# Head norms of the second block's mixer, with the sums of squares made per head on a few partitions instead of per token

## The chip, the cores and the metric

One core of a Trainium2 chip runs one launch of the program. The metric is the device time in microseconds (us), the median of the runs. TensorE is called PE here, VectorE DVE, ScalarE ACT, GpSimd POOL; SP starts most DMAs.

## What is computed

Two transformer blocks of two layers each work on 512 tokens of 1024 features. The second block puts 16 meta tokens ahead (528 positions). Its mixer makes attention with a forget gate (8 heads), a convolution branch and a short convolution branch, and puts their outputs side by side: 1024 features, which are 16 groups ("heads") of 64. Each group is normalized by itself before the output product. The change touches this step alone:

```python
def head_rms_norm(y, g):
    b, l, d = y.shape
    yf = y.astype(jnp.float32).reshape(b, l, d // GROUP_HEAD_DIM, GROUP_HEAD_DIM)
    yf = yf * lax.rsqrt(jnp.mean(yf * yf, axis=-1, keepdims=True) + RMS_EPS)
    return (yf.reshape(b, l, d) * g.astype(jnp.float32)).astype(y.dtype)

def mixer_sublayer(h, pre_g, post_g, w_in, ...):
    ...
    y = jnp.concatenate([y_attn, y_conv, y_sc], axis=-1)
    y = jnp.einsum("ble,ed->bld", head_rms_norm(y, head_g), w_out)
    return h + rms_norm(y, post_g)
```

## The kernel before

Features lie on the partitions (8 tiles of 128 features, called c = 0 to 7, two heads in each), positions on the free axis, in two halves `H[0]` (positions 0 to 271) and `H[1]` (272 to 527). Every projection is made of three products of high and low float32r parts (`mm3`, lines 222 to 224), so PE is the engine with the most work. `mixer2` is called twice, once for each layer. Inside it, `pipeline` walks 20 attention units (scores, softmax, transposes, values); between them `fl.pump` puts in pieces of the projections that are still to be made, and `aux.pump(NORM[i])` puts in pieces of the head norms: `head_norm` is a generator, each of its `yield n` spends n of what a tick allows, and a tick allows 277. After the last unit a loop pumps what is left (`END`). The Tile scheduler then orders the instructions of each engine, so program order is only a start.

The attention outputs are left undivided by their softmax sums (`lrow`): a norm doesn't feel a factor for each token and head, except in its epsilon, so the epsilon is multiplied by the squared sum.

`head_norm(cs, hs)` is called for the tiles [0, 1], [2], [3] (once for each half), [4, 5] and [6, 7]. For each tile and half it squares (`hsq`, line 1423, ACT), and for each block of 128 tokens (and the 16 meta tokens) it takes the *squares as the stationary operand* and two columns of ones, `sel2`, as the moving one (line 1426): the sums arrive in the PSUM bank `x` with tokens on partitions, two columns for each tile. POOL has made `v` (the epsilon times the squared softmax sum, two columns at a time). DVE adds (line 1439), ACT takes the root (1441), DVE the reciprocal `hr` (1443), PE transposes it so that heads lie on partitions (1449), ACT and DVE split it into `rh` and `rl` (1451, 1452), a product with `sel` spreads each head's value over its 64 partitions (1458), and DVE multiplies (1462), ACT and DVE split the result for the output product (1465, 1466). There is one `x` bank: the sums, the transposes, the spread values, and the convolution branch's own products and statistics (1340, 326, 341, 222 with `ah`) follow each other in it. The output product (`out_proj`) of a tile and half begins when `y_done` has it.

Of the kernel before, what the change touches and what calls it, by code (L numbers as in the profile page):

```python
# [9 lines left out]
F32 = mybir.dt.float32  # L10
F32R = mybir.dt.float32r
# [13 lines left out]
RMS = 1e-6  # L25
# [13 lines left out]
MIX = 3  # L39
CT, HN = (260, 720, 617), (100, 160, 277)  # L40
END = (1050, 570)
# [38 lines left out]
def block_stack_kernel(ctx: ExitStack, tc: tile.TileContext, x_in, meta_in, vec_in, lam_in, wup1, wdn1, wqk1,  # L80
# [16 lines left out]

    small_bufs = {"mn": 8, "ls": 4, "rl": 4, "rt": 4, "rt_s": 4, "lf": 1, "lft": 1, "lfe": 1, "nl": 2, "hr": 3, "hv": 3, "lrow": 1, "lrowb": 1, "bl": 1, "bv": 1, "br": 1, "lame": 1}

# [9 lines left out]
    def bank(tag, shape=(128, 512)):  # L109
        return ps.tile(list(shape), F32, tag=tag, bufs=bank_tags[tag], name="ps_" + tag)  # L110
# [17 lines left out]
    epsc = one.tile([128, 2], F32, name="epsc")  # L128
    sel2 = one.tile([128, 2], F32, name="sel2")
    lamc = one.tile([128, 2 * DEPTH], F32, name="lamc")  # L130
# [690 lines left out]
    def mixer1(l, opnd, gpost, nxt):  # L821
        H = HALF[1]
        li = 0.8 - 0.6 * math.exp(-0.3 * l)
        with ExitStack() as st:
# [198 lines left out]
            def subln():  # L1023

                st_ = bank("t")
                for g in range(2):
                    sq = work("bsq")
                    act.activation(out=sq, in_=yb[g][:, T0:TALL], func=ACTF.Square)
                    for tb in range(4):
                        c = 8 * g + 2 * tb  # L1030
                        pe.matmul(out=st_[:, c:c + 2], lhsT=sq[:, tb * 128:tb * 128 + 128], rhs=sel2,
                                  start=True, stop=True)
# [87 lines left out]
    def mixer2(l, opnd, gpost, nxt):  # L1120
        H = HALF[2]
        TB = [(0, 16), (16, 144), (144, 272), (272, 400), (400, 528)]
        with ExitStack() as st:
# [285 lines left out]
            def head_norm(cs, hs):  # L1409

                while 2 * len(sel) < len(cs):
# [3 lines left out]
                    sel.append(t)  # L1415
                blocks = [(h, a, b) for h in hs for a, b in h.tb + ([(0, 128)] if h.meta else [])]
                nb, m = len(blocks), 2 * len(cs)
                stt = bank("x")
                v = small([128, 24], "hv")
                for i, c in enumerate(cs):  # L1420
                    for h in hs:
                        sq = half(name="hsq")
                        act.activation(out=sq[:, h.c], in_=Y(c)[:, h.g], func=ACTF.Square)
                        for j, (hb, a, b) in enumerate(blocks):
                            if hb is h:
                                pe.matmul(out=stt[:, m * j + 2 * i:m * j + 2 * i + 2], lhsT=sq[:, a - h.g0:b - h.g0],
                                          rhs=sel2, start=True, stop=True)
                    for j, (hb, a, b) in enumerate(blocks):

                        vo = v[:, m * j + 2 * i:m * j + 2 * i + 2]  # L1430
                        if c < 4:
                            qb = 0 if a == 0 else (a - 16) // 128 + 1
                            lq = lrow[:, 10 * c + qb:10 * c + qb + 6:5]
                            pool.tensor_scalar(out=vo, in0=lq, scalar1=RMS ** 0.5, scalar2=None, op0=ALU.mult)
                            pool.tensor_tensor(out=vo, in0=vo, in1=vo, op=ALU.mult)
                        else:
                            pool.memset(vo, RMS)
                yield HN[0] * len(cs)
                dve.scalar_tensor_tensor(out=v[:, :m * nb], in0=stt[:, :m * nb], scalar=1.0 / 64, in1=v[:, :m * nb],
                                         op0=ALU.mult, op1=ALU.add)  # L1440
                act.activation(out=v[:, :m * nb], in_=v[:, :m * nb], func=ACTF.Sqrt)
                r = small([128, 24], "hr")
                dve.reciprocal(out=r[:, :m * nb], in_=v[:, :m * nb])
                for h in hs:
                    rt = bank("x")
                    for j, (hb, a, b) in enumerate(blocks):
                        if hb is h:
                            n = 16 if a == 0 else 128
                            pe.transpose(rt[0:m, a - h.g0:a - h.g0 + n], r[0:n, m * j:m * j + m], ident[0:n, 0:n])
                    rh, rl = half(F32R, "rh"), half(F32R, "rl")  # L1450
                    act.activation(out=rh[0:m, h.c], in_=rt[0:m, h.c], func=ACTF.Copy)
                    dve.tensor_tensor(out=rl[0:m, h.c], in0=rt[0:m, h.c], in1=rh[0:m, h.c].bitcast(F32),
                                      op=ALU.subtract)
                    yield HN[1]
                    for i, c in enumerate(cs):
                        rb = bank("x")
                        for j, x in enumerate((rh, rl)):
                            pe.matmul(out=rb[:, h.c], lhsT=sel[i // 2][0:m, i % 2 * 128:i % 2 * 128 + 128],
                                      rhs=x[0:m, h.c], start=j == 0, stop=j == 1)
# [86 lines left out]

    pool.memset(onec, 1.0)
    pool.memset(zeroc, 0.0)
    pool.memset(epsc[:, 0:1], RMS)
# [13 lines left out]
    def load_rest(g0):  # L1563
# [4 lines left out]
        nc.scalar.dma_start(out=xT[:, :, 0:T0], in_=meta_in)  # L1568
        nc.scalar.dma_start(out=sel2, in_=c_selc[:, 8:10])
        cm = half(name="cm")  # L1570
# [220 lines left out]
```

## Time and profile before

| | |
|---|---|
| median of 3 runs | 3471.83 us (3468.62 to 3478.4) |
| profiled execution, its own time | 3497.96 us |
| span of the profiled execution | 3496.2 us, 56247 instructions |
| mean clock granted to TensorE | 0.971 of full speed |
| DMA | 291.42 MB, mean 83 GB/s |

The span is the time from the first to the last instruction; the 1.8 us between it and the execution's own time lie around it. The profiled execution is 26.1 us above the median of the runs. The clock is a share of 2.4 GHz: 1.00 is that level, 0.50 is 1.2 GHz, and a value between them is a stretch that had both.

### The profile page before, as it was taken

How to read it: one execution, taken by the hardware profiler on the slowest of the kernel's cores; microseconds unless marked ns; L12 is line 12 of the kernel's file. 1: busy time of each engine (PE TensorE's matmuls, PEld its weight loads, DVE VectorE, ACT ScalarE, POOL GpSimd, SP SyncE). 2: the span in 40 equal slices, each digit the busy share in tenths (PEclk: the TensorE clock that was granted, in tenths of full speed). 3: DMA queues.
4: the chain of work that ended last, by engine and by line, in shares of the span. 5: the costliest groups of instructions: out<-in, count | busy, mean ns of one | idle time of the engine just before them, and what ended most of it. 6: DMA issues, size and time to landing. Idle time of an engine off the chain costs nothing.

```text
span 3496.2 us, 56247 instructions
## 1 busy us (share of the span) xinstructions
PE 3447.2 (99%) x21851; PEld 3058.9 (87%) x21851; DVE 2033.9 (58%) x4429; ACT 1523.8 (44%) x3336; POOL 32.6 (1%) x147
## 2 busy tenths in 40 slices
PE   9999999999999999999999999999999999999998
PEld 8888988988898888878888898889999988899998
DVE  5442788744345432987644267548774486467743
ACT  6332566623244333666533344545443344554432
POOL 0000000000000000000000000000000000000000
PEclk9999999999999999999999999869999998799999
DMA  4233222232323332222223322102222221022222
GB/s 145 94 93 97 79 73 64 85 97 93 93 80 104 96 91 88 76 79 67 91 91 95 94 84 71 43 31 92 91 91 89 76 92 40 31 82 94 91 91 80
DMA packets 165819, 291.42 MB, mean 83 GB/s; under 512 B 19456, under 2 KB 36896, under 8 KB 165552
## 3 DMA queue, kind: packets, MB, share of 16 engines
q1 hardware_dynamic: 163648, 287.13, 26.2%
q8 instruction: 172, 2.82, 0.3%
q10 hardware_dynamic: 1904, 0.70, 0.1%
q14 instruction: 95, 0.78, 0.1%
HBM read 285.62 MB, written 2.13 MB: 82 GB/s over the span
## 4 chain that ended last, share of the span: by engine, by line
PE 89%; DVE 8%; ACT 2%; issue 1%; DMA 1%; SPq 0%; POOLq 0%; DVEq 0%; ACTq 0%
PE ps_acc L222 10%; PE ps_acc L224 10%; PE ps_acc L223 10%; PE ps_s L223 8%; PE ps_s L222 8%; PE ps_s L224 8%; PE ps_x L222 4%; PE ps_x L223 4%; PE ps_x L224 4%; PE ps_o L223 4%; PE ps_o L222 4%; PE ps_o L224 4%; PE ps_o L813 2%; PE ps_s L796 2%; DVE wl L201 1%; DVE y L1327 1%
## 5 line engine op out<-in xcount | busy, mean ns | idle before, releaser
L200 ACT ACTIVATE wh<-wr 128x512 fp32r<-128x512 f32 (+2 forms) x1068 | 616.9, 615 | 1110.9 <-PE ps_acc L223 488.2
L201 DVE TENSOR_TENSOR wl<-wr,wh 128x512 fp32r<-128x512 f32 (+2 forms) x1068 | 693.4, 673 | 470.2 <-ACT wh L200 457.9
L222 PE MATMUL ps_acc<-xh,wh 128*128 128x256 f32 (+2 forms) x1600 | 541.2, 338 | 1.1 <-DVE y L1303 0.7
L224 PE MATMUL ps_acc<-xh,wl 128*128 128x256 f32 (+2 forms) x1600 | 529.7, 331 | 0.0
L223 PE MATMUL ps_acc<-xl,wh 128*128 128x256 f32 (+2 forms) x1600 | 529.0, 331 | 0.0
L223 PE MATMUL ps_s<-xl,wh 128*128 128x512 f32 (+3 forms) x1088 | 360.6, 331 | 2.3 <-DVE xl L283 0.7
L222 PE MATMUL ps_s<-xh,wh 128*128 128x512 f32 (+3 forms) x1088 | 357.9, 329 | 0.9 <-DVE z L531 0.6
L224 PE MATMUL ps_s<-xh,wl 128*128 128x512 f32 (+3 forms) x1088 | 357.1, 328 | 0.0
L222 PEld LDWEIGHTS ps_acc<-xh,wh 128*128 128x128 f32 x1600 | 313.6, 196 | 30.6 <-issue 3.2
L224 PEld LDWEIGHTS ps_acc<-xh,wl 128*128 128x128 f32 x1600 | 313.9, 196 | 26.2 <-issue 0.8
L223 PEld LDWEIGHTS ps_acc<-xl,wh 128*128 128x128 f32 x1600 | 314.0, 196 | 22.7 <-issue 0.4
L223 PEld LDWEIGHTS ps_s<-xl,wh 128*128 128x128 f32 x1088 | 204.7, 188 | 25.5 <-DVE xl L378 5.2
L222 PEld LDWEIGHTS ps_s<-xh,wh 128*128 128x128 f32 x1088 | 204.7, 188 | 22.4 <-DVE z L531 1.1
L224 PEld LDWEIGHTS ps_s<-xh,wl 128*128 128x128 f32 x1088 | 204.7, 188 | 19.5 <-DVE wl L201 0.2
L222 PE MATMUL ps_x<-xh,wh 128*128 128x256 f32 (+3 forms) x608 | 204.8, 337 | 0.0
L223 PE MATMUL ps_x<-xl,wh 128*128 128x256 f32 (+3 forms) x608 | 202.4, 333 | 0.0
L224 PE MATMUL ps_x<-xh,wl 128*128 128x256 f32 (+3 forms) x608 | 202.0, 332 | 0.0
L223 PE MATMUL ps_o<-xl,wh 128*128 128x512 f32 (+3 forms) x544 | 180.0, 331 | 1.5
L222 PE MATMUL ps_o<-xh,wh 128*128 128x512 f32 (+3 forms) x544 | 177.8, 327 | 0.1
L224 PE MATMUL ps_o<-xh,wl 128*128 128x512 f32 (+3 forms) x544 | 177.5, 326 | 0.0
L223 PE MATMUL ps_acc<-hl,wh 128*128 128x256 f32 (+1 forms) x528 | 168.7, 319 | 0.0
L224 PE MATMUL ps_acc<-hh,wl 128*128 128x256 f32 (+1 forms) x528 | 168.3, 319 | 0.0
(348 smaller groups left out, 7672.5 us busy)
## 6 DMA issues: line engine op xcount, KB each, us to landing
wr<-in_wup_dram SPq DMA_DIRECT2D x528, 256.0 KB, 2.8
wr<-in_wdn_dram SPq DMA_DIRECT2D x192, 256.0 KB, 2.7
wr<-in_wqk_dram SPq DMA_DIRECT2D x96, 256.0 KB, 2.7
wr<-in_wdn_dram SPq DMA_DIRECT2D x96, 192.0 KB, 2.7
wr<-in_wo_dram SPq DMA_DIRECT2D x64, 256.0 KB, 2.7
wr<-in_wv_dram SPq DMA_DIRECT2D x40, 256.0 KB, 2.8
wr<-in_wcv_dram SPq DMA_DIRECT2D x40, 256.0 KB, 2.8
dec<-fdram SPq DMA_DIRECT2D x16, 264.0 KB, 4.4
```

The lines of the kernel that those rows point to most:

```text
L200: act.activation(out=hi[:, a:b], in_=raw[:, :b - a], func=ACTF.Copy)
L201: eng.tensor_tensor(out=lo[:, a:b], in0=raw[:, :b - a], in1=hi[:, a:b].bitcast(F32), op=ALU.subtract)
L222: pe.matmul(out=o, lhsT=wh[wsl], rhs=xh[xsl], start=start, stop=False)
L223: pe.matmul(out=o, lhsT=wh[wsl], rhs=xl[xsl], start=False, stop=False)
L224: pe.matmul(out=o, lhsT=wl[wsl], rhs=xh[xsl], start=False, stop=stop)
L796: pe.matmul(out=o, lhsT=a[R, qs], rhs=b[R, ks], start=j == 0, stop=j == 2 and mask is None)
L813: pe.matmul(out=o[:, q0:], lhsT=v, rhs=p[j], start=kb == 0 and j == 0, stop=kb == n - 1 and j == 1)
L1327: dve.scalar_tensor_tensor(out=y[:, s:], in0=t[0][:, :TALL - s], scalar=w[:, 30 - s:31 - s], in1=y[:, s:], op0=ALU.mult, op1=ALU.add))
```

## The change

Sums with heads on partitions. The squares are now the *moving* operand: `selz` is a tile of 16 columns, zero but for the two columns of ones in the middle, and a slice of it that begins at column 7 - 2i puts the sums of tile i of a call on rows 2i and 2i + 1 of the `x` bank, for all 272 (or 256) positions of a half in one product (line 1430); the other rows get zeros added. For the attention tiles, `v` (now one DVE instruction, 64 times the epsilon times the squared sums) is transposed and added in the same bank by a product with the identity, for each block of tokens (1434). ACT takes the root of that row block of up to 4 x 272 values out of PSUM, with 1/64 as scale and, for the tiles without softmax sums, the epsilon as bias (1436); DVE takes the reciprocal of those 4 x 272 values (1438); `rh` and `rl` are split from it (1440, 1441). The add on DVE, the transposes of the reciprocals and all of POOL's work on `v` are gone. `HN` is (277, 277, 277): each piece of a norm spends a whole tick. All squares of a call come in the first piece, then one piece for each half up to `rl`, and only then the spread products.

```diff
-CT, HN = (260, 720, 617), (100, 160, 277)
+CT, HN = (260, 720, 617), (277, 277, 277)
...
-                                pe.matmul(out=stt[:, m * j + 2 * i:m * j + 2 * i + 2], lhsT=sq[:, a - h.g0:b - h.g0],
-                                          rhs=sel2, start=True, stop=True)
...
-                            pool.tensor_scalar(out=vo, in0=lq, scalar1=RMS ** 0.5, scalar2=None, op0=ALU.mult)
-                            pool.tensor_tensor(out=vo, in0=vo, in1=vo, op=ALU.mult)
-                        else:
-                            pool.memset(vo, RMS)
-                yield HN[0] * len(cs)
-                dve.scalar_tensor_tensor(out=v[:, :m * nb], in0=stt[:, :m * nb], scalar=1.0 / 64, in1=v[:, :m * nb],
-                                         op0=ALU.mult, op1=ALU.add)
-                act.activation(out=v[:, :m * nb], in_=v[:, :m * nb], func=ACTF.Sqrt)
-                r = small([128, 24], "hr")
-                dve.reciprocal(out=r[:, :m * nb], in_=v[:, :m * nb])
+                m, attn, sqs, rr = 2 * len(cs), cs[0] < 4, {}, {}
+                if attn:
+
+                    v, lq = small([128, 20], "hv"), lrow[:, 10 * cs[0]:10 * cs[0] + 5 * m]
+                    dve.scalar_tensor_tensor(out=v[:, 0:5 * m], in0=lq, scalar=64.0 * RMS, in1=lq, op0=ALU.mult,
+                                             op1=ALU.mult)
                 for h in hs:
-                    rt = bank("x")
-                    for j, (hb, a, b) in enumerate(blocks):
-                        if hb is h:
-                            n = 16 if a == 0 else 128
-                            pe.transpose(rt[0:m, a - h.g0:a - h.g0 + n], r[0:n, m * j:m * j + m], ident[0:n, 0:n])
-                    rh, rl = half(F32R, "rh"), half(F32R, "rl")
-                    act.activation(out=rh[0:m, h.c], in_=rt[0:m, h.c], func=ACTF.Copy)
-                    dve.tensor_tensor(out=rl[0:m, h.c], in0=rt[0:m, h.c], in1=rh[0:m, h.c].bitcast(F32),
+                    for c in cs:
+                        sqs[c, h.i] = half(name="hsq")
+                        act.activation(out=sqs[c, h.i][:, h.c], in_=Y(c)[:, h.g], func=ACTF.Square)
+                yield HN[0]
+                for h in hs:
+                    ms, r = bank("x"), half(name="hr")
+                    for i, c in enumerate(cs):
+                        pe.matmul(out=ms[0:m, h.c], lhsT=selz[:, 7 - 2 * i:7 - 2 * i + m], rhs=sqs[c, h.i][:, h.c],
+                                  start=i == 0, stop=not attn and c == cs[-1])
+                    blocks = [(j, max(a, h.lo), b) for j, (a, b) in enumerate(TB) if h.lo <= a < h.hi]
+                    for j, a, b in blocks if attn else []:
+                        pe.matmul(out=ms[0:m, a - h.g0:b - h.g0], lhsT=v[:b - a, j:5 * m:5], rhs=ident[:b - a, :b - a],
+                                  start=False, stop=j == blocks[-1][0])
+                    act.activation(out=r[0:m, h.c], in_=ms[0:m, h.c], func=ACTF.Sqrt, scale=1.0 / 64,
+                                   bias=0.0 if attn else epsc[0:m, 0:1])
+                    dve.reciprocal(out=r[0:m, h.c], in_=r[0:m, h.c])
+                    rh, rl = rr[h.i] = half(F32R, "rh"), half(F32R, "rl")
+                    act.activation(out=rh[0:m, h.c], in_=r[0:m, h.c], func=ACTF.Copy)
+                    dve.tensor_tensor(out=rl[0:m, h.c], in0=r[0:m, h.c], in1=rh[0:m, h.c].bitcast(F32),
                                       op=ALU.subtract)
                     yield HN[1]
+                for h in hs:
                     for i, c in enumerate(cs):
                         rb = bank("x")
-                        for j, x in enumerate((rh, rl)):
+                        for j, x in enumerate(rr[h.i]):
...
+    pool.memset(selz, 0.0)
...
-        nc.scalar.dma_start(out=sel2, in_=c_selc[:, 8:10])
+        nc.scalar.dma_start(out=selz[:, 7:9], in_=c_selc[:, 8:10])
```

What moves, at three places of the first layer's mixer. The first is PE at the norm of the convolution tiles [4, 5]; before, its ten products of two columns (line 1426) stand in this piece of the order, among a unit's transposes and scores (L1285, L1288, L1291 transposes, L796 scores, L813 values).

```order
L1288 MATMUL ps_t<-ident,sc 16x16
L1426 MATMUL ps_x<-sel_84,hsq 128x2 x8
L1291 MATMUL ps_t<-ident,sc 128x128
L796 MATMUL ps_s<-ql,qh 128x400 x2
L1426 MATMUL ps_x<-sel_84,hsq 128x2 x2
L813 MATMUL ps_o<-pt,v 128x256 x8
```

In the changed kernel the sums of its first half stand earlier, among products of a projection (L222 to L224); those of the second half follow twenty rows below.

```order
L222 MATMUL ps_acc<-xh,wh 128x256
L1430 MATMUL ps_x<-hsq,selz 4x272
L1285 MATMUL ps_o<-ident,sc 16x128
L1430 MATMUL ps_x<-hsq,selz 4x272
L223 MATMUL ps_acc<-xl,wh 128x256
L224 MATMUL ps_acc<-xh,wl 128x256
L796 MATMUL ps_s<-qh 128x272 x2
```

Eight products in a row have become two, with a transpose between them.

The second place is PE at the norm of the tiles [0, 1]. Before, the transposes of the reciprocals (L1449) stand behind the scores of a unit.

```order
L796 MATMUL ps_s<-qh,ql 128x272 x2
L1449 MATMUL ps_x<-ident,hr 4x128 x2
L1449 MATMUL ps_x<-ident,hr 4x16
L813 MATMUL ps_o<-pt,v 128x272
L813 MATMUL ps_s<-pt,v 128x272
L796 MATMUL ps_s<-qh 128x256
L326 MATMUL ps_x<-onec,lacc 128x1 x3
```

In the changed kernel the sums of the second half (L1430, L1434), the convolution branch's transposes (L341, L343) and the first spread product (L1448) follow each other here in the one `x` bank.

```order
L1430 MATMUL ps_x<-hsq,selz 4x256 x2
L1434 MATMUL ps_x<-ident,hv 4x128 x2
L813 MATMUL ps_o<-pt,v 128x272 x2
L813 MATMUL ps_s<-pt,v 128x272 x2
L796 MATMUL ps_s<-qh 128x256
L341 MATMUL ps_x<-ident,R 128x128 x2
L343 MATMUL ps_x<-ident,R_21975 128x16
L813 MATMUL ps_o<-pt,v 128x256
L796 MATMUL ps_s<-ql,qh 128x256
L796 MATMUL ps_s<-qh,ql 128x256
L813 MATMUL ps_s<-pt,v 128x256
```

PE no longer waits for the reciprocal there; it asks for the `x` bank three times within a dozen rows.

The third place is DVE at the same norm, in the changed kernel alone (before, the reciprocal of 128 x 20 values stood between a unit's score reductions): the reciprocal of the second half stands ahead of the multiplication L1358, which reads the transposes L341 out of the `x` bank.

```order
L201 TENSOR_TENSOR wl<-wr,wh 128x512
L1438 RECIPROCAL hr<-hr 4x256
L1358 TENSOR_TENSOR y<-y,ps_x 128x272 x2
L1441 TENSOR_TENSOR rl<-hr,rh 4x256
L1298 TENSOR_TENSOR pt<-ps_t,pt 128x2x128 x2
```

So the bank is given up only behind that reciprocal.

On ACT the order of the changed kernel has 72 loads of a function table where that of before has 70.

## Rows read from the trace of the kernel before

**Rows 1.** The page, parts 1 and 4: busy time of each engine; the chain.
```profile
PE 3447.2 (99%) x21851; PEld 3058.9 (87%) x21851; DVE 2033.9 (58%) x4429; ACT 1523.8 (44%) x3336; POOL 32.6 (1%) x147
...
PE 89%; DVE 8%; ACT 2%; issue 1%; DMA 1%; SPq 0%; POOLq 0%; DVEq 0%; ACTq 0%
```
**Rows 2.** Windows: stretch, length, busy time of each engine, clock, DMA share, GB/s.
```profile
2112.00:2346.00 234.00, 221.71 (x1361) 190.47 (x1359) 134.48 (x375) 112.74 (x290) 12.25 (x62) 0.80 0.14 45
2834.00:3067.00 233.00, 220.65 (x1365) 189.57 (x1364) 135.08 (x377) 112.62 (x291) 12.13 (x61) 0.79 0.14 45
400.00:680.00 280.00, 275.61 (x1959) 240.39 (x1958) 232.59 (x610) 176.13 (x452) 0.00 (x0) 0.99 0.23 71
```
**Rows 3.** Windows: stretches of the second block's mixers, columns as in rows 2.
```profile
2222.00:2251.00 29.00, 26.64 (x117) 22.90 (x117) 13.85 (x42) 14.99 (x31) 0.41 (x2) 0.59 0.06 19
...
2265.00:2274.00 9.00, 9.00 (x48) 7.58 (x47) 1.74 (x9) 4.05 (x10) 0.97 (x13) 0.62 0.17 57
...
2283.00:2313.00 30.00, 30.00 (x129) 25.02 (x129) 12.98 (x40) 11.62 (x26) 0.41 (x2) 0.54 0.08 24
...
2319.00:2345.00 26.00, 22.84 (x96) 19.26 (x97) 7.77 (x20) 7.73 (x20) 0.00 (x0) 0.55 0.00 1
...
2988.00:2999.00 11.00, 11.00 (x59) 8.97 (x60) 2.91 (x11) 5.45 (x17) 1.56 (x16) 0.69 0.15 49
...
3005.00:3035.00 30.00, 29.95 (x130) 24.76 (x130) 13.15 (x42) 12.00 (x29) 0.41 (x2) 0.55 0.06 18
```
**Rows 4.** Timeline of PE: start, length, line, operands, shape, count.
```profile
2265.26 2.01 PE L1426 MATMUL ps_x<-sel,hsq 128*128 128x2 f32 x16
...
2283.72 0.51 PE L1426 MATMUL ps_x<-sel,hsq 128*128 128x2 f32 x4
...
2284.45 0.41 PE L224 MATMUL ps_acc<-xh,wl 128*128 128x256 f32 x1
```
**Rows 5.** Windows: the first block's mixer, a stretch of its first layer.
```profile
562.00:568.00 6.00, 6.00 (x36) 5.58 (x37) 4.31 (x16) 3.30 (x7) 0.00 (x0) 0.72 0.24 87
```
**Rows 6.** Groups of instructions, PE: count, busy us, mean ns, idle before.
```profile
L1426 PE MATMUL ps_x<-sel,hsq 128*128 128x2 f32 x160 | 23.0, 260 | 1.5 <-ACT hsq L1423 1.4
L1449 PE MATMUL ps_x<-ident,hr 128*4 128x128 f32 (+3 forms) x50 | 11.7, 324 | 5.5 <-DVE hr L1443 2.4 <-DVE y L1358 1.9 <-DVE y L1462 1.2
L1340 PE MATMUL ps_x<-y,onesm 128*128 128x272 f32 (+1 forms) x16 | 4.8, 399 | 0.0
L1031 PE MATMUL ps_t<-sel,bsq 128*128 128x2 f32 x32 | 4.2, 254 | 0.0
```
**Rows 7.** Waits of PE, both layers: us in total, times, longest.
```profile
PE ps_x L1449 <- DVE hr L1443: 2.4, 2, 1.2
...
PE ps_x L1449 <- DVE y L1358: 1.9, 2, 1.0
PE ps_x L1458 <- DVE rl L1452: 1.9, 2, 0.9
...
PE ps_x L1458 <- DVE y L1462: 1.2, 2, 0.6
PE ps_x L1449 <- DVE y L1462: 1.2, 2, 0.6
```
**Rows 8.** Groups of instructions, DVE, 2210 to 2350 us.
```profile
L1452 DVE TENSOR_TENSOR rl<-ps_x,rh 4x272 fp32r<-4x272 f32 x3 | 1.3, 429 | 3.4 <-ACT rh L1451 3.4
...
L1443 DVE RECIPROCAL hr<-hv 128x20 f32<-128x20 f32 x3 | 0.8, 274 | 0.3 <-ACT hv L1441 0.3
...
L1443 DVE RECIPROCAL hr<-hv 128x4 f32<-128x4 f32 x1 | 0.2, 178 | 0.3 <-ACT hv L1441 0.3
```
**Rows 9.** Timeline of ACT at the norm of the tiles [0, 1].
```profile
2217.92 0.22 ACT L1441 ACTIVATE hv<-hv 128x20 f32<-128x20 f32 x1 [1.37 <-DVE hv L1439]
2218.16 1.28 ACT L1241 ACT_TABLE_LOAD   x1
...
2220.73 0.39 ACT L1451 ACTIVATE rh<-ps_x 4x272 fp32r<-4x272 f32 x1 [0.55 <-PE ps_x L1449]
```

More of the change, by code (lines that the diff above doesn't have):

```diff
@@ L96, in half @@
         return hp.tile([128, HB], dt, tag="h", name=name)
-    small_bufs = {"mn": 8, "ls": 4, "rl": 4, "rt": 4, "rt_s": 4, "lf": 1, "lft": 1, "lfe": 1, "nl": 2, "hr": 3, "hv": 3, "lrow": 1, "lrowb": 1, "bl": 1, "bv": 1, "br": 1, "lame": 1}
+    small_bufs = {"mn": 8, "ls": 4, "rl": 4, "rt": 4, "rt_s": 4, "lf": 1, "lft": 1, "lfe": 1, "nl": 2, "hv": 3, "lrow": 1, "lrowb": 1, "bl": 1, "bv": 1, "br": 1, "lame": 1}
     def small(shape, name="sm"):
@@ L128, in block_stack_kernel @@
     epsc = one.tile([128, 2], F32, name="epsc")
-    sel2 = one.tile([128, 2], F32, name="sel2")
+    selz = one.tile([128, 16], F32, name="selz")
     lamc = one.tile([128, 2 * DEPTH], F32, name="lamc")
@@ L1030, in subln @@
                         c = 8 * g + 2 * tb
-                        pe.matmul(out=st_[:, c:c + 2], lhsT=sq[:, tb * 128:tb * 128 + 128], rhs=sel2,
+                        pe.matmul(out=st_[:, c:c + 2], lhsT=sq[:, tb * 128:tb * 128 + 128], rhs=selz[:, 7:9],
                                   start=True, stop=True)
@@ L1415, in head_norm @@
                     sel.append(t)
[L1416 to L1423, printed above, removed]
-                        for j, (hb, a, b) in enumerate(blocks):
-                            if hb is h:
-                                pe.matmul(out=stt[:, m * j + 2 * i:m * j + 2 * i + 2], lhsT=sq[:, a - h.g0:b - h.g0],
-                                          rhs=sel2, start=True, stop=True)
[L1428 to L1433, printed above, removed]
-                            pool.tensor_scalar(out=vo, in0=lq, scalar1=RMS ** 0.5, scalar2=None, op0=ALU.mult)
-                            pool.tensor_tensor(out=vo, in0=vo, in1=vo, op=ALU.mult)
-                        else:
-                            pool.memset(vo, RMS)
@@ L1438, in head_norm @@
-                yield HN[0] * len(cs)
-                dve.scalar_tensor_tensor(out=v[:, :m * nb], in0=stt[:, :m * nb], scalar=1.0 / 64, in1=v[:, :m * nb],
-                                         op0=ALU.mult, op1=ALU.add)
-                act.activation(out=v[:, :m * nb], in_=v[:, :m * nb], func=ACTF.Sqrt)
-                r = small([128, 24], "hr")
-                dve.reciprocal(out=r[:, :m * nb], in_=v[:, :m * nb])
-                for h in hs:
-                    rt = bank("x")
-                    for j, (hb, a, b) in enumerate(blocks):
-                        if hb is h:
-                            n = 16 if a == 0 else 128
-                            pe.transpose(rt[0:m, a - h.g0:a - h.g0 + n], r[0:n, m * j:m * j + m], ident[0:n, 0:n])
-                    rh, rl = half(F32R, "rh"), half(F32R, "rl")
-                    act.activation(out=rh[0:m, h.c], in_=rt[0:m, h.c], func=ACTF.Copy)
-                    dve.tensor_tensor(out=rl[0:m, h.c], in0=rt[0:m, h.c], in1=rh[0:m, h.c].bitcast(F32),
+                m, attn, sqs, rr = 2 * len(cs), cs[0] < 4, {}, {}
```

## The prediction

> **What bounds the kernel now.** I read the page first. PE is busy 99% of the span and carries 89% of the chain that ended last; DVE is busy 58%, ACT 44%, POOL 1% [rows 1]. So time comes out of PE's own work, out of its waits, or out of its clock, and work on DVE or ACT costs only where PE ends up waiting for it. The windows then show where PE is slow although it is busy. The two mixers of the second block take 234 and 233 us and had a granted clock of 0.80 and 0.79, while the first block's mixer, with the same kind of attention, had 0.99 [rows 2]. A stretch at 0.50 does half of its products; with PE busy, a stretch loses its length times (1 - clock): 234 x 0.20 + 233 x 0.21 = 95.7 us over both layers. That is much more than PE waits for there, and the head norms lie in just these stretches.
>
> Which stretches are they? In the first layer 2222 to 2251 (0.59), 2265 to 2274 (0.62), 2283 to 2313 (0.54) and 2319 to 2345 (0.55); the second layer repeats the middle two at 2988 (0.69) and 3005 (0.55) [rows 3]. In the first and the last of them PE has 2 to 3 us without work. In the middle two it has none: 9.00 of 9.00 and 30.00 of 30.00 us are busy. What PE did ahead of these is the burst of sums with two moving columns: sixteen passes from 2265.26, and the last four of another from 2283.72; a projection's product at 2284.45 is already at 0.41 us, the half-clock length [rows 4]. The first block has such sums too, line 1031, 32 passes in both layers [rows 6], and the one slow stretch of its first mixer, 562 to 568 at 0.72, lies right behind its share of them [rows 5]. I read from this that a row of products which move two columns each ends with the clock at 1.2 GHz, with no wait needed.
>
> **The change, part by part.** *PE's own work.* A float32 product appears as two passes in the trace, a transpose as one. Before, the sums are 160 passes with 23.0 us busy and the transposes 50 with 11.7 us [rows 6]: 34.7 us go. What comes: 16 tile-halves a layer, 32 products, 64 passes of 272 or 256 moving columns. Line 1340 moves the same columns in float32: 4.8 us for 16 passes, 0.30 each [rows 6], so 64 x 0.30 = 19.2 us. The stationary side has 4 columns instead of 128 there; I know of no row that prices this, and take no gain. And 30 products of `v` with the identity, 60 passes, 48 of them of 128 columns and 12 of 16. From below, 0.30 x 128 / 264 = 0.145 each, 8.7 us; from above the transposes of line 1449, which move 128 columns too, mostly at half clock: 11.7 / 50 = 0.234, 14.0 us. I take the middle, 11.4. Sum: 30.6 - 34.7 = -4 us. The bounds are -7 and, with the removed sums at the full-clock price of line 1031 (4.2 / 32 = 0.131, so 21.0 in place of 23.0), +1.
>
> *ACT.* 20 roots of 272 or 256 columns in place of 12 short ones. The nearest row of that width is `rh`, 0.39 us; a short root took 0.22 [rows 9]: 20 x 0.39 - 12 x 0.22 = +5.2 us, and two more table loads at 1.28 [rows 9] make +7.8. On an engine that is busy 112.7 of 234 us there [rows 2] this costs nothing by itself; without cover it would cost 7.8 us, which is inside the bound of the waits below. The root out of PSUM is also what frees the `x` bank.
>
> *DVE.* 20 reciprocals of 272 or 256 columns in place of 12 of 4 to 20. A reciprocal took 274 ns for 20 columns and 178 for 4 [rows 8], 6.0 ns a column, so about 178 + 268 x 6.0 = 1.79 us for 272 whatever the number of partitions. The other end is the subtraction in that shape, 0.43 us [rows 8], if the slope ended; I take 1.79, since the slope is between two rows of this very instruction. DVE gains about 20 x 1.74 - 12 x 0.25 = +32 us over both layers, at 57% busy in the mixers [rows 2]: hidden as work. What queues behind each reciprocal is hidden only if PE has something else to do.
>
> A rule of the Trainium skill speaks against this edit: by its page "VectorE: DVE Perf Modes", section "First, the fixed hardware budget", the reciprocal is an iterative division with a repeat count of 8. With the clock of 0.96 GHz of that page's "Specifications" this is an estimate of 272 x 8 / 0.96 = 2.27 us, where the slope of the rows gives 1.79. By the page DVE would gain 42 us instead of 32, and the slow case below would come out some 9 us later. The rows agree that the price goes with the columns and not with the partitions; they show a smaller step.
>
> *Waits.* Gone are PE's waits ahead of the transposes, 2.4 + 1.9 + 1.2 = 5.5 us in both layers [rows 7]. The chain from sums to `rl` is now root 0.39, reciprocal 1.79, `rh` 0.39, `rl` 0.43, 3.0 us, against 0.22 + 0.27 + 0.39 + 0.43 = 1.3 and the transposes [rows 8, 9], so up to 1.7 us longer, twenty times. Since each step of a norm now has a tick of its own, most have products of a projection in between. Where not: at the norm of [0, 1] the second half's sums, the branch's transposes and a spread product share the `x` bank within a dozen rows, and on DVE the reciprocal stands ahead of the multiplication that empties the bank. That is 1.7 + 2 x 0.43 = 2.6 us, with four products in between, at 0.41 us or less each [rows 4]: 1 to 2 us of wait, I take 1.5. At [4, 5] and at [2] the sums of the second half need the bank that the root of the first half still reads, with a table load of 1.28 us ahead of it; I take 1 us each, and 1 us at the norm of [6, 7] at the end: 4.5 a layer, 9 in all, less 5.5, +3.5 us. From below nothing new: -5.5. From above all twenty chains uncovered by 1.7 us: 34 - 5.5 = +28.5.
>
> POOL's `v` instructions go; nothing but the norm waited for them, so nothing changes there.
>
> *The clock.* With the bursts gone, the two middle stretches of each layer need not fall: 9 x 0.38 + 30 x 0.46 + 11 x 0.31 + 30 x 0.45 = 34.1 us is what they lose [rows 3]. But once the clock is down there it stays so through a mixture of values, transposes and spread products without a wait, and the new waits of about 1 us lie at the same places. No row shows what a stream of 272 columns past 4 stationary ones does to the clock. I take half, -17 us, between 0 and -34.
>
> **Sum.** -4 + 3.5 - 17 = -17.5 us. On the profiled execution's own 3497.96 us that is 3480; that execution lies 26 us above the median of the runs, 3471.83, on which the forecast is made: 3454 us.
>
> **Rivals.** *The clock falls all the same.* The waits at [4, 5] and [2] take the place of the bursts. The stretch 2222 to 2251, behind waits for the norm of [0, 1], speaks for it; against it, that only 1 us is meant to wait there. Time: -4 + 3.5, 3471 us.
>
> *The reciprocals hold PE up (slower).* One mechanism: reciprocals of 1.7 us on DVE between the sums and the next use of the one `x` bank. With no gain of clock and all chains uncovered: 28.5 - 4 = +24, 3496 us. It decides from 1.0 us uncovered per chain: 20 x 1.0 - 5.5 - 4 = +10.5. For it: one bank, and a DVE order that puts the reciprocal ahead of the instruction that frees it. Against it: DVE idles 43% of these stretches and the longer chain often has ten or more products beside it.
>
> *The clock holds nearly throughout.* If the streams keep it up, the stretches around 2222 and 2319 (29 x 0.41 + 26 x 0.45 = 23.6 us, doubled for the second layer 47) may shorten by half too: -34 - 24 + 3.5 - 4 = -58, 3414 us. Against it: these two have real waits, and the output product's last tile still needs its norm.
>
> **How the numbers follow.** 0.3%, 10.4 us, is about what a measurement of this kernel can tell from no change. Chances: the forecast (3440 to 3465) 0.36, the clock falls all the same 0.26, the reciprocals 0.26, the clock holds 0.12. Faster: most of the first and all of the last, 0.46; within 0.3%: most of the second with the edges of the first and third, 0.27; slower 0.27. The 80% range reaches into the last case and nearly to the full price of the reciprocals: 3420 to 3492 us.
>
> **What would show it.** Right: the sums as 64 passes of about 0.3 us or less; reciprocals near 1.8 us; no wait of PE for a reciprocal ahead of a transpose; clock well above 0.62 and 0.54 behind the norms of [4, 5] and [2]; PE waits of 1 us or so at the `x` bank for the root (1436) or for multiplications behind a reciprocal. Wrong: a clock of the mixers still near 0.80 (then the bursts were not the cause, or the waits have replaced them), or PE waits above 20 us in all on the norm's lines (then the reciprocal is the bound).

## The result, and the profile after

The changed kernel takes 3436.8 us (median of 4 runs, 3436.42 to 3440.26), beside 3475.11 for the kernel before on the same chip: a ratio of 0.989, 95% interval 0.986 to 0.992, or 38 us less. It is faster; the forecast was 3454, and 3436.8 lies 3 us below the forecast case's own 3440 to 3465 and inside the range of 3420 to 3492. The gain is twice the forecast one, 38 us for 17.5.

The page of the changed kernel, parts 1 and 4:

```profile
span 3434.7 us, 55936 instructions
...
PE 3384.3 (99%) x21765; PEld 2995.1 (87%) x21765; DVE 2061.5 (60%) x4433; ACT 1530.6 (45%) x3346; POOL 8.6 (0%) x28
...
PE 88%; DVE 8%; ACT 2%; issue 1%; DMA 1%; SPq 0%; POOLq 0%; DVEq 0%; ACTq 0%
```

PE is the bound as before [rows 1], and it is without work for 3434.7 - 3384.3 = 50.4 us of the span, against 3496.2 - 3447.2 = 49.0 before. So the waits have not become fewer. The windows show where the time came from: both mixers, then four stretches of the first.

```profile
2099.00:2309.00 210.00, 198.68 (x1377) 164.42 (x1376) 156.76 (x394) 119.28 (x302) 0.13 (x1) 0.94 0.17 53
2800.00:3001.00 201.00, 189.10 (x1288) 155.20 (x1288) 146.39 (x375) 114.94 (x294) 0.00 (x0) 0.93 0.16 52
2205.00:2231.00 26.00, 24.36 (x169) 18.75 (x167) 18.61 (x54) 22.80 (x51) 0.00 (x0) 1.00 0.06 21
2231.00:2240.00 9.00, 7.94 (x43) 6.92 (x42) 5.45 (x15) 5.71 (x14) 0.00 (x0) 0.62 0.19 60
2240.00:2296.00 56.00, 52.50 (x358) 39.77 (x354) 42.09 (x97) 38.88 (x92) 0.13 (x1) 1.00 0.12 38
2296.00:2307.00 11.00, 10.15 (x38) 8.22 (x38) 4.69 (x12) 4.07 (x12) 0.00 (x0) 0.54 0.00 0
```

The mixers' clock is 0.94 and 0.93 where it was 0.80 and 0.79 [rows 2]. The two stretches in the middle, behind the norms of [4, 5] and [2], which were at 0.62 and 0.54 [rows 3], are gone: 2240 to 2296 is at 1.00. What is left of long half-clock stretches in this mixer comes behind waits: 2231 to 2240 behind the waits of the convolution branch's products for the `x` bank and for their operand `al`, 2296 to 2307 behind those at the mixer's end. By length times (1 - clock) the mixers now lose 210 x 0.06 + 201 x 0.07 = 26.7 us, where they lost 95.7.

The profiled execution before was a long one (3497.96 us), so these two profiles differ by more than the medians do. For all runs there is a number that takes the clock out: span x mean granted clock is what the span would be at 2.4 GHz throughout, and the rest of it is what the clock took. The clock is given to three decimals, so one run is known to 2 us, a mean to about 1.

| kernel | median us | ratio to before, 95% | span x clock, mean | taken by the clock, mean |
|---|---|---|---|---|
| before (21 runs) | 3474.9 | | 3397 | 78 |
| changed | 3436.8 | 0.986 to 0.992 | 3396 | 40 |
| E1 before, products regrouped | 3481.8 | 0.999 to 1.003 | 3397 | 81 |
| E2 before, products 128 wide | 3443.7 | 0.988 to 0.992 | 3397 | 45 |
| E3 changed + narrow products | 3463.4 | 0.994 to 0.998 | 3412 | 49 |
| E4 changed + wide products | 3447.3 | 0.989 to 0.993 | 3410 | 36 |
| E5 changed + narrow, earlier | 3466.8 | 0.995 to 0.999 | 3412 | 52 |
| E6 before, new ticks | 3453.2 | 0.992 to 0.996 | 3391 | 62 |
| E7 changed, 3 reciprocals | 3496.3 | 1.004 to 1.008 | 3420 | 74 |
| E8 changed, line 1031 wide | 3437.1 | 0.988 to 0.992 | 3395 | 41 |
| E9 changed, old ticks | 3443.9 | 0.988 to 0.994 | 3391 | 52 |
| E10 before, wide, new ticks | 3439.0 | 0.987 to 0.993 | 3396 | 42 |
| E11 changed, no reciprocals | 3416.9 | 0.980 to 0.986 | 3388 | 26 |
| E12 changed, rows split | 3440.2 | 0.986 to 0.992 | 3402 | 35 |

Each ratio is to runs of the kernel before made beside that kernel's own; E12 ran on another chip than E1 to E11. The first two rows are the result: work and waits together 1 us less, the clock 38 us. The kernel before ran between 3465 and 3500 us at clocks of 0.982 to 0.970, and its span x clock stayed between 3391 and 3402, without a trend: most of its spread, too, is the clock.

The groups of the norm's products on PE, changed kernel:

```profile
L1430 PE MATMUL ps_x<-hsq,selz 128*4 128x272 f32 (+3 forms) x64 | 18.2, 386 | 2.8 <-ACT hsq L1425 1.4 <-ACT rt_s L328 0.9 <-ACT hr L1436 0.5
L1448 PE MATMUL ps_x<-rh,sel 4*128 4x272 f32 (+3 forms) x32 | 13.4, 420 | 7.3 <-ACT hr L1436 3.3 <-DVE y L1452 3.1 <-DVE y L1358 0.6
L1448 PE MATMUL ps_x<-rl,sel 4*128 4x272 f32 (+3 forms) x32 | 10.4, 324 | 0.0
L1434 PE MATMUL ps_x<-ident,hv 128*2 128x128 f32 (+3 forms) x60 | 8.3, 253 | 0.0
```

The sums are 64 passes at 0.284 us, the products of `v` 60 at 0.138: 26.5 us for the 34.7 that went. The waits that are new stand at the spread products, 3.3 us for the root and 3.1 for the multiplication, all at the two mixers' ends. The timeline there, all engines:

```profile
2290.07 1.28 ACT L1436 ACT_TABLE_LOAD   x1
2291.37 0.48 ACT L1436 ACTIVATE hr<-ps_x,epsc 4x272 f32<-4x272 f32 x1
2291.88 1.84 DVE L1438 RECIPROCAL hr<-hr 4x272 f32<-4x272 f32 x1 [1.85 <-ACT hr L1436]
...
2293.76 0.43 ACT L1440 ACTIVATE rh<-hr 4x272 fp32r<-4x272 f32 x1 [1.91 <-DVE hr L1438]
2294.09 0.45 ACT L1436 ACTIVATE hr<-ps_x,epsc 4x256 f32<-4x256 f32 x1
...
2294.57 1.74 DVE L1438 RECIPROCAL hr<-hr 4x256 f32<-4x256 f32 x1
2294.59 0.39 PE L1448 MATMUL ps_x<-rh,sel 4*128 4x272 f32 x1 [1.67 <-ACT hr L1436]
...
2296.24 0.38 DVE L1452 SCALAR_TENSOR_TENSOR y<-y,vec,ps_x 128x272 f32<-128x272 f32 x1
...
2296.68 0.59 PE L1448 MATMUL ps_x<-rh,sel 4*128 4x272 f32 x1 [1.58 <-DVE y L1452]
```

Both waits name a short instruction, and both are a reciprocal's. The first reciprocal holds `rh` on ACT, and the second half's root stands behind `rh`; only then is the `x` bank free, at 2294.54. The second reciprocal stands on DVE ahead of the multiplication that frees the bank again. Half clock begins at 2296, behind the first of these waits and within the second.

### The profile page after: what moved, and what is told of

It is laid out like the page before. It is cut to its first block, busy times and chain, and to the rows that moved or that the text cites. A ratio compares the mean times of both kernels' runs of the same rounds, so it can differ in the third digit from the quotient of the medians.

```text
span 3434.7 us, 55936 instructions
## 1 busy us (share of the span) xinstructions
PE 3384.3 (99%) x21765; PEld 2995.1 (87%) x21765; DVE 2061.5 (60%) x4433; ACT 1530.6 (45%) x3346; POOL 8.6 (0%) x28
## 4 chain that ended last, share of the span: by engine, by line
PE 88%; DVE 8%; ACT 2%; issue 1%; DMA 1%; SPq 0%; POOLq 0%; DVEq 0%; ACTq 0%
PE ps_acc L222 10%; PE ps_acc L223 10%; PE ps_acc L224 10%; PE ps_s L223 8%; PE ps_s L222 8%; PE ps_s L224 8%; PE ps_x L222 4%; PE ps_x L223 4%; PE ps_x L224 4%; PE ps_o L223 4%; PE ps_o L222 4%; PE ps_o L224 4%; PE ps_o L813 2%; PE ps_s L796 1%; DVE wl L201 1%; DVE y L1327 1%
## 5 line engine op out<-in xcount | busy, mean ns | idle before, releaser
L222 PE MATMUL ps_acc<-xh,wh 128*128 128x256 f32 (+2 forms) x1600 | 530.5, 332 | 1.1 <-DVE y L1303 0.7
L224 PE MATMUL ps_acc<-xh,wl 128*128 128x256 f32 (+2 forms) x1600 | 519.2, 324 | 0.0
L223 PE MATMUL ps_acc<-xl,wh 128*128 128x256 f32 (+2 forms) x1600 | 518.1, 324 | 0.0
L222 PE MATMUL ps_s<-xh,wh 128*128 128x512 f32 (+3 forms) x1088 | 357.1, 328 | 3.1 <-DVE z L531 2.1
L224 PE MATMUL ps_s<-xh,wl 128*128 128x512 f32 (+3 forms) x1088 | 356.5, 328 | 0.2 <-DVE wl L201 0.2
L222 PEld LDWEIGHTS ps_acc<-xh,wh 128*128 128x128 f32 x1600 | 304.3, 190 | 29.6 <-issue 2.3
L224 PEld LDWEIGHTS ps_acc<-xh,wl 128*128 128x128 f32 x1600 | 303.9, 190 | 25.7 <-issue 1.1
L223 PEld LDWEIGHTS ps_acc<-xl,wh 128*128 128x128 f32 x1600 | 304.5, 190 | 23.4 <-issue 1.4
L222 PEld LDWEIGHTS ps_s<-xh,wh 128*128 128x128 f32 x1088 | 204.7, 188 | 23.2 <-DVE z L531 2.5
L224 PEld LDWEIGHTS ps_s<-xh,wl 128*128 128x128 f32 x1088 | 204.5, 188 | 18.9 <-DVE wl L201 0.4
L222 PE MATMUL ps_x<-xh,wh 128*128 128x256 f32 (+3 forms) x608 | 204.3, 336 | 0.0
L224 PE MATMUL ps_x<-xh,wl 128*128 128x256 f32 (+3 forms) x608 | 201.7, 332 | 0.0
L222 PE MATMUL ps_o<-xh,wh 128*128 128x512 f32 (+3 forms) x544 | 177.5, 326 | 0.1
L224 PE MATMUL ps_o<-xh,wl 128*128 128x512 f32 (+3 forms) x544 | 177.3, 326 | 0.0
L222 PE MATMUL ps_acc<-hh,wh 128*128 128x256 f32 (+1 forms) x528 | 168.1, 318 | 0.0
```

The source lines that it names most:

```text
L222: pe.matmul(out=o, lhsT=wh[wsl], rhs=xh[xsl], start=start, stop=False)
L223: pe.matmul(out=o, lhsT=wh[wsl], rhs=xl[xsl], start=False, stop=False)
L224: pe.matmul(out=o, lhsT=wl[wsl], rhs=xh[xsl], start=False, stop=stop)
```

## The experiments

Theory: the products of the sums that move two columns (line 1426) make the granted clock fall, and taking them away is the gain. Rivals: the new pieces of the order (the ticks, no transposes, no work on POOL) took waits away; PE has less work.

**E1 and E2: the kernel before, with its products widened.** E1 is the control: the squares first, then the products block by block, two columns each.

```diff
...
+                for j, (hb, a, b) in enumerate(blocks):
+                    for i in range(len(cs)):
+                        pe.matmul(out=stt[:, m * j + 2 * i:m * j + 2 * i + WID], lhsT=sqs[i, hb.i][:, a - hb.g0:b - hb.g0],
+                                  rhs=selw[:, 0:WID], start=True, stop=True)
...
```

E1 has `WID = 2`, E2 `WID = 128`; `selw` is the two columns of ones with the identity behind them.

> The kernel before, with a norm's squares all made first and its two-column products then issued block by block; the same 80 products, two columns each. It is the control of the next run. Both theories: 3474 us, within 10 us of before, mixers' clock near 0.80 as before. If it already gains 15 us or more, the order of the products, not their shape, was the cause.

> As the control, but each of the 80 products moves 128 columns instead of 2 (the first two are the columns of ones, what the other 126 leave in the bank is overwritten by the next product or never read). The weight load of 128 columns (144 ns a pass before) should still set the pace, so PE's own work grows by at most 80 x 2 x some 20 ns = 3 us; all waits, transposes and POOL's work stay. Theory clock (a run of products with two moving columns is what the granted clock falls behind): the mixers' clock rises from 0.80 to above 0.90 and the time falls by 20 to 38 us against the control, to about 3445. Theory waits (the removed transposes, POOL work and pieces of the order made the gain): within 5 us of the control. Theory PE work: 0 to 3 us slower.

E1 took 3481.8 us, no change. E2 took 3443.7: 38 us less than E1, 31 less than before. The mixers by windows, of E1 and then of E2, and the group of the products in E1 and in E2:

```profile
2110.00:2343.00 233.00, 221.97 (x1380) 190.61 (x1379) 136.74 (x380) 114.13 (x293) 13.07 (x62) 0.80 0.15 45
2832.00:3064.00 232.00, 219.62 (x1355) 188.58 (x1354) 134.12 (x374) 112.62 (x290) 12.20 (x61) 0.79 0.15 45
```

```profile
2099.00:2320.00 221.00, 210.73 (x1467) 182.95 (x1466) 147.59 (x399) 114.89 (x301) 12.38 (x63) 0.91 0.17 53
2800.00:3017.00 217.00, 207.41 (x1442) 179.75 (x1441) 144.92 (x394) 111.70 (x296) 12.23 (x61) 0.91 0.17 51
```

```profile
L1428 PE MATMUL ps_x<-selw,hsq 128*128 128x2 f32 x160 | 22.9, 263 | 1.5 <-ACT hsq L1425 1.4
```

```profile
L1428 PE MATMUL ps_x<-selw,hsq 128*128 128x128 f32 x160 | 21.8, 285 | 0.2
```

One number differs between the two kernels, the width of the moving operand. The 160 passes cost the same (22.9 and 21.8 us), the work the same (3397 us both), and the clock takes 45 us in place of 81. The transposes, POOL's work and the old ticks are all still there. So the two columns are what costs 36 us of clock here, and neither rival explains this. It does not follow that every row of such products brings the clock down: see E3 and E5.

**E3 to E5: the narrow products put back into the changed kernel.** E3 issues them in front of the streamed sums of a call's first half, into columns that nobody reads; E5 one piece earlier, into a bank of its own; E4 issues 40 more streams in their place.

```diff
+                    if h is hs[0]:
+                        o = 300
+                        for hb in hs:
+                            for c in cs:
+                                for a, b in hb.tb + ([(0, 128)] if hb.meta else []):
+                                    pe.matmul(out=ms[:, o:o + 2], lhsT=sqs[c, hb.i][:, a - hb.g0:b - hb.g0],
+                                              rhs=selz[:, 7:9], start=True, stop=True)
+                                    o += 2
```

> The changed kernel, with the 80 two-column products of before put back as idle work in front of the streamed sums, into columns 300 and up of the same bank that nobody reads. PE's work grows by the 23.0 us that they took before. Theory clock: the clock behind norms [4, 5] and [2] falls again to 0.5 to 0.7, mixers near 0.82, and the time grows by 23 + 20 to 38 us, to 3480 to 3498. Theories waits and PE work: by 23 us alone, to 3460, clock of the mixers 0.93 as in the changed kernel.

> The changed kernel with 40 more streamed sums (272 or 256 columns), each written where the true sums then start afresh: 80 passes of some 0.29 us, 23 us of PE work as in the run with idle two-column products. All theories: 3455 to 3463 us, mixers' clock 0.92 to 0.95. What the other run takes beyond this one is due to the shape of the products.

> The changed kernel with the same 80 idle two-column products as in the run before, but one piece earlier, behind the squares and into a bank of their own, so that a unit's transposes, scores and values follow them (as before the change) and not the streamed sums. Theory that what follows a burst decides how long the clock stays down: 3470 to 3485, half-clock stretches of 10 us and more behind norms [4, 5] and [2], as in the kernel before. Theory that the number of such products alone decides: 3458 to 3468, as with the burst directly ahead of the sums.

E3 took 3463.4, E4 3447.3. Both added some 15 us of work and waits (expected: 23; part of it fills PE's waits: PE idles 45.6 us in E3 and 44.2 in E4, against 50.4). By time E3 came out at the rivals' 3460, not at the theory's 3480 to 3498, and E4 below its 3455 to 3463. What is left for the theory is the comparison of the two: E3 lost 13 us more to the clock than E4, so the shape of the products counts here too, but for less than the 20 to 38 us that I expected. E3's dips are short. Windows of the norm of [4, 5] in E3, then its timeline there:

```profile
2244.00:2248.00 4.00, 4.00 (x33) 3.55 (x32) 1.96 (x6) 2.04 (x10) 0.00 (x0) 1.00 0.39 131
2248.00:2252.00 4.00, 4.00 (x19) 2.73 (x18) 2.44 (x7) 3.94 (x6) 0.00 (x0) 0.57 0.00 0
2252.00:2299.00 47.00, 46.24 (x318) 36.75 (x317) 32.78 (x75) 28.84 (x67) 0.13 (x1) 1.00 0.10 35
```

```profile
2244.82 1.95 PE L1434 MATMUL ps_x<-selz,hsq 128*128 128x2 f32 x16
...
2247.47 0.51 PE L1434 MATMUL ps_x<-selz,hsq 128*128 128x2 f32 x4
```

Sixteen narrow passes, no idle time, and half clock behind them, as in [rows 4]; but it is over by 2252, where the kernel before stayed there for 9 and then 30 us [rows 3]. The ten narrow passes of the norm of [2], from 2267.03 on, lie in the third window, at 1.00: behind them the clock did not fall at all. I thought that what follows a burst decides this. E5, with a unit's transposes and values behind the bursts, took 3466.8: inside the other theory's 3458 to 3468. Its trace says more than its time. The bursts of [4, 5] and of [2] start at 2252.26 and 2269.66, and no half clock follows either in the first mixer:

```profile
2252.00:2290.00 38.00, 37.66 (x262) 29.89 (x260) 25.65 (x62) 21.87 (x54) 0.00 (x0) 1.00 0.14 42
```

So my theory fell. The other one, that the number of such products alone decides, does not hold either: the same 80 cost some 36 us of clock in the kernel before (E1 against E2) and 9 to 12 here (49 and 52 against 40).

**E6, E9, E10: the table of ticks.** E6 is the kernel before with `HN = (277, 277, 277)`; E9 the changed kernel with the old `(100, 160, 277)`; E10 is E2 with the new table.

> The kernel before with only the table of ticks changed to (277, 277, 277). Theory clock by narrow products: 3465 to 3485, within 10 us of before, mixers' clock about 0.80. Theory waits (the pieces' new places made the gain): 3450 or less.

> The changed kernel with the old table of ticks (100, 160, 277). Narrow products and the table have each been taken out of the kernel before by itself (3444 with wide products, 3453 with the table, from 3475). If the two are separate costs, the table is worth some 20 us here too: 3450 to 3460. If the table helped only because it spread the bursts of narrow products, it is worth little where there are none: 3436 to 3446.

> The kernel before with both: its 80 products widened to 128 columns, and the new table of ticks. Sums still with tokens on partitions, transposes and POOL's work as before. If the two are separate costs: 3453 - 31 = 3422, faster than the changed kernel. If they share one cost (bursts bunched in one place): 3436 to 3444, about the changed kernel.

| sums | old ticks | new ticks |
|---|---|---|
| narrow products | 3474.9 (before) | 3453.2 (E6) |
| 128 wide, tokens on partitions | 3443.7 (E2) | 3439.0 (E10) |
| streamed, heads on partitions | 3443.9 (E9) | 3436.8 (changed) |

E6 was a miss: I gave the table 10 us at most, and it is worth 22 alone, 16 of it by the clock and 6 by work and waits. But where no product is narrow it is worth 5 to 7. For the most part the two take the same loss away. Windows of E6, first mixer and its middle:

```profile
2110.00:2324.00 214.00, 203.26 (x1377) 176.30 (x1376) 137.06 (x380) 111.97 (x292) 13.09 (x62) 0.87 0.16 50
...
2271.00:2275.00 4.00, 4.00 (x20) 3.48 (x20) 1.38 (x6) 1.98 (x4) 0.00 (x0) 0.57 0.23 66
2275.00:2305.00 30.00, 29.54 (x226) 26.00 (x224) 19.66 (x54) 19.73 (x46) 0.89 (x5) 1.00 0.11 36
```

With the pieces a whole tick apart, the dip behind the narrow products of [2] ends after 4 us, and the next 30 us are at full clock. In the kernel before they were not [rows 3]. The two columns of the table also say that moving the heads to partitions is worth nothing beside the wide products: 0 with the old ticks, 2 us with the new ones, which the measurement can't tell from nothing.

**E7 and E11: the price of the reciprocals.** E7 takes two more in each chain, E11 none.

```diff
-                    dve.reciprocal(out=r[0:m, h.c], in_=r[0:m, h.c])
+                    r2 = half(name="hr2")
+                    dve.reciprocal(out=r2[0:m, h.c], in_=r[0:m, h.c])
+                    dve.reciprocal(out=r2[0:m, h.c], in_=r2[0:m, h.c])
+                    dve.reciprocal(out=r[0:m, h.c], in_=r2[0:m, h.c])
```

> The changed kernel with three reciprocals in a row where it has one (the second undoes the first): each of the 20 chains is 2 x 1.8 = 3.6 us longer, DVE has 72 us more. If the reciprocals are hidden as I forecast: only the two chains at a mixer's end show, 2 x 2 x (1.8 to 3.6) with the clock behind them, 3442 to 3455. Rival that reciprocals hold PE up (from 1.0 us uncovered on each chain): 20 x 3.6 = 72 us, 3490 to 3510.

> The changed kernel without its 20 reciprocals of 1.74 to 1.84 us: the roots themselves are split and spread, so the outputs are scaled wrongly. If the reciprocals are hidden but for the mixers' ends, where PE waits 3.3 us on each for rows that stand behind them: 2 x 3.3 and the half clock of some 11 us behind them (5 us lost each): 3420 to 3432. If they are hidden altogether: 3434 to 3438. If each chain is uncovered, as the run with three of them suggests (58 us for 72): 29 us less, 3405 to 3415.

E7 took 3496.3, 60 us more than the changed kernel; I had expected 5 to 18. E11 took 3416.9, 20 us less. So the reciprocals are not hidden. PE's waits in both mixers, of E7 and then of E11:

```profile
PE ps_x L1451 <- ACT rh L1443: 21.0, 8, 3.2
PE ps_x L1451 <- ACT hr L1436: 5.5, 2, 2.8
```

```profile
PE ps_x L1447 <- DVE y L1451: 1.7, 2, 0.9
...
PE ps_x L1430 <- ACT hr L1436: 1.1, 2, 0.6
```

In E11 the ends' waits of 3.3 and 3.1 us have shrunk to 1.7. In E7 eight spread products wait up to 3.2 us each. By the table above, the 60 us of E7 are 24 of work and waits and 35 of clock, and the 20 us of E11 are 8 and 13. Where is that clock? The two mixers, of E7 and then of E11:

```profile
2110.00:2337.00 227.00, 197.47 (x1288) 160.41 (x1287) 177.37 (x394) 117.37 (x293) 0.13 (x1) 0.86 0.15 46
2830.00:3054.00 224.00, 195.59 (x1287) 159.82 (x1287) 177.16 (x394) 117.08 (x292) 0.00 (x0) 0.88 0.16 47
```

```profile
2100.00:2301.00 201.00, 193.27 (x1338) 160.81 (x1338) 138.46 (x377) 114.40 (x298) 0.13 (x1) 0.93 0.18 55
2790.00:2984.00 194.00, 187.23 (x1322) 154.46 (x1320) 135.51 (x373) 113.83 (x296) 0.00 (x0) 0.96 0.18 55
```

By length times (1 - clock) E7 loses 58.7 us there, 32 more than the changed kernel's 26.7: nearly all of the 35. So in E7 the waits cost more by the half clock behind them than by themselves. E11 loses 21.8, 5 less than the changed kernel, so only 5 of its 13 us are seen in the mixers, which hold all twenty reciprocals; where the rest comes from stays open.

E11 also shows the clock fall where there is neither a narrow product of these sums nor a wait just ahead; spread products on 4 rows and values on 16 rows come before it:

```profile
2246.00:2252.00 6.00, 6.00 (x37) 3.72 (x36) 4.72 (x13) 4.93 (x11) 0.00 (x0) 1.00 0.31 87
2252.00:2259.00 7.00, 7.00 (x29) 5.38 (x27) 2.65 (x8) 4.54 (x12) 0.00 (x0) 0.51 0.01 2
```

**E8: the same products in the first block.** Line 1031 widened to 128 columns, as in E2.

> The changed kernel, and in the first block the 32 two-column products of the sub-layer norm (line 1031) widened to 128 columns in the same way. The clock is down for some 4 us behind them in each of the two layers (566 and 1588 us: 1.9 and 1.7 us lost). Theory clock by narrow products: both dips go, 2 to 4 us faster than the changed kernel, 3433 to 3435. Theory that the wait on the chain behind these products makes the dip: no change, 3436 to 3438.

The windows behind line 1031, of the changed kernel and then of E8:

```profile
562.00:570.00 8.00, 8.00 (x50) 7.20 (x50) 4.50 (x17) 5.24 (x10) 0.00 (x0) 0.79 0.19 66
1584.00:1592.00 8.00, 8.00 (x53) 7.46 (x52) 5.63 (x19) 4.35 (x10) 0.00 (x0) 0.79 0.21 66
```

```profile
562.00:570.00 8.00, 8.00 (x68) 7.47 (x67) 5.15 (x19) 6.05 (x12) 0.00 (x0) 1.00 0.22 68
1584.00:1592.00 8.00, 7.49 (x62) 6.76 (x60) 5.93 (x21) 5.78 (x14) 0.00 (x0) 1.00 0.22 66
```

Both dips are gone, in another stage and with the width alone changed. The time, 3437.1 us, shows no gain, nor does what the clock takes (41 us for 40): 3 us are less than these runs tell apart (3434.18 to 3441.89).

**E12: the reciprocals made shorter.** Positions of a half in two blocks on rows of their own, so that the rows are 128 or 144 columns long.

```diff
+                    for b, (p0, p1) in enumerate(cut[h.i]):
+                        for i, c in enumerate(cs):
+                            q = b * nc_ + i
+                            pe.matmul(out=ms[0:M, 0:p1 - p0], lhsT=selz[:, 7 - 2 * q:7 - 2 * q + M],
+                                      rhs=sqs[c, h.i][:, p0:p1], start=q == 0, stop=not attn and q == 2 * nc_ - 1)
...
+                    dve.reciprocal(out=r[0:M, 0:w], in_=r[0:M, 0:w])
...
+                                pe.matmul(out=rb[:, p0:p1], lhsT=sel[q // 2][0:M, q % 2 * 128:q % 2 * 128 + 128],
+                                          rhs=x[0:M, 0:p1 - p0], start=j == 0, stop=j == 1)
```

> The changed kernel with each half's positions in two blocks of 128 (144 with the meta tokens) that stand on rows of their own: 8 rows of 144 columns where 4 of 272 were (4 of 144 for a single tile). Root, reciprocal and split then run over half the columns: a reciprocal of about 1.0 us (6.0 ns a column, as 1839 against 1740 ns for 272 and 256), 0.8 less on each of 20 chains. The price: 64 more passes of sums and 64 more of spread values, each of half the width, at most 64 x 0.2 + 64 x 0.15 = 22 us if they don't get shorter with the width, some 3 if they do. If the reciprocals' length is what PE waits for (20 us for all of it): 3437 - 9 + 3 = 3431, range 3426 to 3436. If shorter products or more of them cost as much: 3437 to 3450.

The instructions by tile in E12 (count; minimum, median, maximum in ns; first and last start; forms), and under them PE's busy time and count on the tiles `rh` and `rl`, 2100 to 3100 us:

```profile
L1445 DVE RECIPROCAL hr<-hr x20: 930/991/1042, 2225.5 to 3000.9; 8x144 f32<-8x144 f32 x6, 8x128 f32<-8x128 f32 x6, 4x144 f32<-4x144 f32 x4, 4x128 f32<-4x128 f32 x4
```

```profile
2100.00:3100.00 1000.00, 18.06 (x64) 0.97 0.24 75
...
2100.00:3100.00 1000.00, 16.33 (x64) 0.97 0.24 75
```

The reciprocals came down as expected, to 0.99 us, the waits at the mixers' ends went, and the clock took 5 us less. But the spread products, twice as many and half as wide, cost 34.4 us in place of 13.4 + 10.4: 3440.2 us, no gain, and outside the 3426 to 3436 that I gave. The sums, also twice as many and half as wide, cost the same as before, 18.3 us for 18.2. No kernel here that makes the whole computation beats the changed one by more than the runs can tell.

## Why the prediction was right, and where it was off

**The sign and its cause were right.** That the narrow products bring the clock down, with PE busy throughout, was read from [rows 3 to 5]; E2 shows by one number that their width costs 36 us of clock. The rule was put too strongly: "ends with the clock at 1.2 GHz" fails in E3 behind [2] and in E5, where the clock stays at 1.00. The rival "the clock falls all the same" is out: it is 1.00 behind [4, 5] and [2].

**The clock term was mis-sized.** "I take half, -17 us, between 0 and -34": the runs give 78 - 40 = 38 us, which is more than all of the middle stretches (34.1). And those 34 us were read from a long execution, which lost 3496.2 x 0.029 = 101 us to the clock where the mean run loses 78. The dips around 2222 and 2319 became shorter as well (2231 to 2240, 2296 to 2307), which was the third rival, and by this mechanism the truth lies between the forecast and it. "Half" stood on the guess that new waits would keep the clock down at [4, 5] and [2]; there are none of them there. The table of ticks had no term in the sum; E6 shows 22 us for it alone.

**PE's own work**: -8.2 us of busy time in place of -4, beyond the bound of -7 (26.5 added where 30.6 was worked out; the passes of `v` came at 0.138, below the lower bound of 0.145). **Waits**: PE idles 1.4 us more; +3.5 was forecast. Part of the work that went had run at half clock, so some of the -8.2 is clock; taken together and with the clock out, by span x clock, the two are -1 us, near the forecast -0.5.

**"Hidden" was wrong for the reciprocals.** Their length was right: 1839 and 1740 ns for 272 and 256 columns, where the slope gave 1.79 us for 272. That partitions don't count was taken from rows that are all on 128; the changed kernel shows it, on 4. The Trainium skill's page "VectorE: DVE Perf Modes", section "First, the fixed hardware budget", led to an estimate of 2.27; the measurement decides for the slope. But E11 shows that 20 such reciprocals cost 20 us, 8 of work and waits and 13 of clock. The 8 are about the 9 us of new waits that the prediction had in its sum; the clock behind such waits had no price there. The rival that reciprocals hold PE up was a true mechanism, at 0.4 us of wait per chain where it would have decided "from 1.0 us uncovered per chain"; the kernel is faster since the clock gave back more.

**The number is in the range, but not for the reasons of the sum.** Two errors of the clock, one in each direction, stood beside each other: the win was taken too small, and a wait was priced at its own length. The first is the larger, so the gain came out twice the forecast; without its reciprocals (E11) the kernel is 58 us below the one before. That the second error took back part of the first is luck.

**What stays open.** What decides whether the clock falls at one place, and for how long. Behind the narrow products of [4, 5] and [2] it was down for 9 and 30 us in the kernel before, some 4 in the windows shown of E3 and E6, and not at all in E3 behind [2] and in E5's first mixer. The narrow products cost 31 us with the old ticks (E2) and 14 with the new (E6 against E10), so the place of the pieces decides, but E5 did not find what about it. And E11's dip at 2252 has no such product ahead of it. What is shown is the cost of narrow products over the whole kernel, not a rule for a single row of them.

## What to carry to other kernels

Sums by a product whose moving operand has two columns can be made with 128 columns for the same PE time; look at the granted clock behind every run of narrow products, also where PE never waits. Where the clock moves, split each run into span x clock and the rest before looking for a cause. Where half clock follows the waits, as in E7, price a wait of PE by itself and by the half clock behind it, and follow an instruction that "frees a bank" back to the long one that stands ahead of it on its engine.

## What the runs showed of the hardware that I had not expected

A pass of 128 moving columns past 128 stationary ones in float32 costs no more than one of two: 21.8 against 22.9 us for 160 (E2, E1), 4.1 against 4.2 for the 32 of line 1031 (E8, changed). Past `sel`, 128 stationary columns on 2 to 8 rows, a pass of 128 to 144 columns is not half of one of 272: the spread values took 34.4 us for 128 passes (E12), 23.8 for 64. Past a slice of `selz`, at most 8 stationary columns, it is: the sums took 18.3 us for 128 passes and 18.2 for 64. The clock fell without an idle gap just ahead (E3, 2244 to 2252, twice 4.00 of 4.00 us busy), and 24 us more of waits and work came with 35 us of half clock (E7). The Trainium skill's page "TensorE: Matmul & The Clock Gate", section "HAM oscillation — how this bites in real kernels", tells of the fall as that of an engine that waits for its data; the dips at 2231 and 2296 of the changed kernel lie behind waits too, of up to 0.7 and 1.7 us for DVE and ACT (the page's wait is one for DMA), while those behind the narrow products and E11's at 2252 have none just ahead.
